# A two-part transformer kernel: norms scaled on ScalarE and transposed on TensorE, conditioning sums in the experts' buffers, and the last norm's row spread through PSUM

## The chip, the cores and the metric

The kernel runs on one core of a Trainium2 chip. The core has five instruction streams that run side by side and wait for each other through semaphores: TensorE (PE in the profile, its weight loads PEld), VectorE (DVE), ScalarE (ACT), GpSimd (POOL) and SyncE (SP, which only issues transfers). Transfers run on 16 DMA engines. TensorE's clock has two levels, 1.2 and 2.4 GHz; the profile gives the granted clock of a stretch as a share of the full one. The metric is device time in microseconds (us) of one execution.

## The reference, cut to what matters

512 tokens of width 1024 go through two stacks, all in float32.

```
first_block:  for l in 0, 1:
    mod = silu(c) @ ada_w[l] + ada_b[l]            # six rows of 1024: shift, scale, gate (twice)
    hn  = rms_norm(h, g) * (1 + scale) + shift
    h   = h + gate * mixer_l(hn)                   # l = 0: gated recurrence, l = 1: stick-breaking attention
    hn  = rms_norm(h, g') * (1 + scale') + shift'
    h   = h + gate' * peer_ffn(hn)
    (after l = 0: keys and values from kv_ada_w, rms_norm and kv_w)
  return rms_norm(h, final_norm_g)

peer_ffn, each token: 64 experts e with weights gates[e], chosen by top-k over product keys
    hid[e] = xn . u[e];   out = sum_e gates[e] * gelu(hid[e]) * v[e]

second_block: hn = rmsnorm(x, g_pre) * (1 + scale) + shift;  proj = hn @ w_in
    mix = [gated_deltanet(proj), sparse_attention(proj)] @ w_out
    x   = x + gate * rmsnorm(mix, g_post)
```

## The kernel before, in words

The tokens are four blocks of 128, one token to a partition; `H[0]` to `H[3]` hold their residual rows of 1024. Stages run over pairs of blocks.

A **conditioning sum** (`ada`, 17 of them in the first 337 us) makes one row of 1024 from `silu(c)` and a 1024x1024 matrix: four loads of 1 MB into the ring of eight `g` buffers (`row2`), a multiply and seven multiply-adds of 128x1024 on DVE into the tile `acc`, of which there is one, and eight matmuls with a column of ones that add over the partitions into PSUM `ax`. DVE adds the bias to it.

A **norm** (`norm_T`, 24 calls: six stages by four blocks) takes the reciprocal root mean square of a block on ACT (`rms`), multiplies the identity by it on DVE (tile `dg`, a diagonal matrix), and multiplies eight 128x128 pieces of the residual by that matrix on PE, which transposes and scales at once. ACT then scales and shifts the pieces out of PSUM into the projections' operand.

A **peer block** (`peer(l, b)`) gathers for each of 64 experts a row of u and v (1 MB for 128 tokens, by GpSimd's indirect transfer, into a `g` buffer), takes the dot product with u on DVE, gelu on ACT for four experts at a time, and adds the weighted v either on DVE (tile `acc`) or on PE (a diagonal `dgv` made on ACT, then two 128x512 matmuls into PSUM `vp`); `PE_SLOTS` says how many go to PE. At the end `acc` and `vp` are added, multiplied by the gate, which is spread over the partitions by diagonals and matmuls with ones into `ax`, and added to `H[b]`. A buffer of the ring comes free for the next gather once its v is used. Each pair of peer blocks is merged with the other stages' work for other blocks: the mixers, the next norms, keys and values, and beside the last pair the second stack for blocks 0, 1 and 2. The second stack of block 3 is the tail.

`spread` puts a gate row on all partitions in the same way as above, with diagonals from DVE. `second_norm` multiplies a block by its root mean square and by the row `final_norm_g`, which is loaded to all partitions by two transfers on SP into two of the six `t2` buffers, and then calls `norm_T`. `dsa_attend` multiplies the softmax numerators by a diagonal of 1/sum on PE, which transposes them.

The order of work on SP is that of the program. The order on the other engines is chosen when the program is built, by a list scheduler, so that moved lines of code don't say by themselves how the engines' orders move.

Of the kernel before, what the change touches and what calls it, by code (L numbers as in the profile page):

```python
# [12 lines left out]
I32 = mybir.dt.int32  # L13
# [7 lines left out]
D = 1024  # L21
KC = 8
NB = 4
# [14 lines left out]
PE_SLOTS = {(0, 0): 16, (0, 1): 32, (0, 2): 28, (0, 3): 24, (1, 0): 24, (1, 1): 24, (1, 2): 20, (1, 3): 24}  # L38
# [71 lines left out]
def kernel(ctx: ExitStack, tc: tile.TileContext, a, at, out):  # L110
# [163 lines left out]
    def norm_T(src, ga, sh, dst, t0, wide=None):  # L274

        r = rms(src, D)
        dg = S("dg" if wide is None else "dgv", [128, 128], bufs=3 if wide is None else 2)
        ts(dg, ident, r, OP.mult)
        yield
        for half in range(2):  # L280
            p = mmt() if wide is None else wide[:, half * 512:half * 512 + 512]
            for j in range(4):
                k = 4 * half + j
                mm(p[:, j * 128:(j + 1) * 128], src[:, k * 128:(k + 1) * 128], dg)
            for j in range(4):
                k = 4 * half + j
                act(dst[:, k, t0:t0 + 128], p[:, j * 128:(j + 1) * 128], AF.Identity,
                    scale=ga[:, k:k + 1], bias=sh[:, k:k + 1])
            yield
# [31 lines left out]
    def ada(cact, name, i, bias, dst):  # L321

        acc = S("acc", [128, D], bufs=ACC_BUFS)
        for k in range(KC):
            if k % 2 == 0:
                two = row2().rearrange("p (j n) -> p j n", j=2)
                loads[-1].dma_start(two, a[name][i, k * 128:k * 128 + 256].rearrange("(j p) n -> p j n", p=128))
            w = two[:, k % 2]
            if k:
                stt(acc, w, cact[:, k:k + 1], acc, OP.mult, OP.add)  # L330
            else:
                ts(acc, w, cact[:, 0:1], OP.mult)
            yield
        p = axt()
        for j in range(8):
            mm(p[:, j:j + 1], acc[:, j * 128:j * 128 + 128], one)
        tt(dst, p[:, :8], bias, OP.add)
        yield

    def spread(cols, dst):  # L340

        for half in range(2):
            p = axt()
            for j in range(4):
                dg = S("dg", [128, 128], bufs=3)
                ts(dg, ident, cols[:, 4 * half + j:4 * half + j + 1], OP.mult)
                mm(p[:, j * 128:(j + 1) * 128], C["ones"], dg)
            A.copy(dst[:, half * 512:half * 512 + 512], p)
            yield

# [200 lines left out]
    def route_pick(l, b, qT, xT, kb, m=4):  # L551
# [7 lines left out]
        idx = S("idx", [128, 4, 16], I32, bufs=3)  # L559
        gt = S("gt", [128, 4, 16], bufs=3)  # L560
# [83 lines left out]
    def peer(l, b, cols):  # L644
# [3 lines left out]
        on_pe = [((e + 1) * npe) // 64 > (e * npe) // 64 for e in range(64)]  # L648
        hid = S("hid", [128, 64], bufs=2)
# [4 lines left out]
        rows = {}  # L654
        for s in range(64 + GROUP):
            if s < 64:
# [8 lines left out]
            e = s - GROUP  # L665
            if e < 0:
                yield
                continue
            if e % GROUP == 0:
                g = slice(e, e + GROUP)  # L670
                tt(w[:, g], w[:, g], gt[:, g], OP.mult)
            t = rows.pop(e)[:, D:]
            if on_pe[e]:
                dg = S("dgv", [128, 128], bufs=2)
                act(dg, ident, AF.Copy, scale=w[:, e:e + 1])
                left -= 1
                for half in range(2):
                    sl = slice(half * 512, half * 512 + 512)
                    mm(vp[:, sl], dg, t[:, sl], first_p, left == 0)
                first_p = False  # L680
            elif first_d:
                ts(acc, t, w[:, e:e + 1], OP.mult)
                first_d = False
            else:
                stt(acc, t, w[:, e:e + 1], acc, OP.mult, OP.add)
            yield
        if (l, b) == (1, NB - 1):
            for half in range(2):
                sl = slice(half * 512, half * 512 + 512)
                tt(acc[:, sl], acc[:, sl], vp[:, sl], OP.add)  # L690
        else:
            tt(acc, acc, vp, OP.add)
        for half in range(2):
            sl = slice(half * 512, half * 512 + 512)
            p = axt()
            for j in range(4):
                dg = S("dg", [128, 128], bufs=3)
                act(dg, ident, AF.Copy, scale=cols[:, 4 * half + j:4 * half + j + 1])
                mm(p[:, j * 128:(j + 1) * 128], C["ones"], dg)
            tt(acc[:, sl], acc[:, sl], p, OP.mult)  # L700
# [127 lines left out]
    def second_norm(b, t0, hT):  # L828
        fg = [t2(), t2()]
        for half in range(2):  # L830
            sl = slice(half * 512, half * 512 + 512)
            SP.dma_start(fg[half], a["final_norm_g"][sl].unsqueeze(0).to_broadcast([128, 512]))
        r = rms(H[b], D)
        for half in range(2):
            sl = slice(half * 512, half * 512 + 512)
            stt(H[b][:, sl], H[b][:, sl], r, fg[half], OP.mult, OP.mult)
# [133 lines left out]
    def dsa_attend(b, d, qbT, zbs, mix):  # L970
        N = 128 * (b + 1)
        for h in range(4):
# [17 lines left out]
            dg = S("dg", [128, 128], bufs=3)  # L990
            ts(dg, ident, s, OP.mult)
            yield
            p = pot()
            for j in range(b + 1):
                mm(p[:, j * 128:(j + 1) * 128], l[:, j * 128:(j + 1) * 128], dg)
# [467 lines left out]
def lay(inputs):  # L1463
# [21 lines left out]
    for n, src in (("c", "c"), ("c_2", "c_2"), ("norm_mix_g", "norm_mix_g"), ("lb", "hgrn_lb_logits"),  # L1485
                   ("onorm", "hgrn_onorm_g"), ("norm_ffn_g", "norm_ffn_g"), ("kv_ada_b", "kv_ada_b"),
                   ("kv_norm_g", "kv_norm_g"), ("b_ada_2", "b_ada_2"), ("g_pre", "g_pre_2"), ("ada_b", "ada_b"),
                   ("g_post", "g_post_2"), ("conv", "conv_w_2"), ("g_gdn", "g_gdn_2")):
# [31 lines left out]
```

## Time and profile before

| | us |
|---|---|
| median of 3 runs | 2449.67 (2448.4 to 2451.24) |
| the profiled execution | 2450.95 |
| its span | 2449.2 |
| PE busy | 1882.7 (77%) |
| DVE busy | 1786.6 (73%) |
| ACT busy | 758.7 (31%) |
| POOL busy | 673.8 (28%) |

The mean granted clock of TensorE is 0.871. Busy is the time in which an engine executed something, over the whole program; the 767 MB that the transfers moved are 313 GB/s on average. Six stretches are told apart below by time: 0 to 312 us, before the first gather; 312 to 798, with peer blocks (0,0) and (0,1); 798 to 1222, with (0,2) and (0,3); 1222 to 1658, with (1,0) and (1,1); 1658 to 2290, with (1,2), (1,3) and the second stack of blocks 0 to 2; and the tail.

### The profile page before, as it was taken

The numbers are of one execution on the slowest core, as the hardware profiler recorded it, in microseconds if no ns is written. First come the engines' busy times: TensorE is split into PE (matmuls) and PEld (weight loads), VectorE is DVE, ScalarE is ACT, GpSimd is POOL, SyncE is SP. The second block draws the span as 40 slices with busy tenths as digits, with TensorE's granted clock in tenths as the row PEclk, the third lists the DMA queues.
The fourth block names the chain that finished last, engine by engine and source line by source line (L and its number), as shares of the span: only waits on it lengthen the run. The fifth ranks groups of instructions, "written<-read, shape, count | busy, mean of one in ns | idle before, by whom it ended". The sixth has DMA issues, their size and how long they took to land.

```text
span 2449.2 us, 25291 instructions
## 1 busy us (share of the span) xinstructions
PE 1882.7 (77%) x8832; PEld 1375.8 (56%) x8832; DVE 1786.6 (73%) x3772; ACT 758.7 (31%) x1601; POOL 673.8 (28%) x516
## 2 busy tenths in 40 slices
PE   5996859977945997784489887547996788974698
PEld 4984748853721784462168565315774465742484
DVE  5677887789698737879862786996768656777573
ACT  2331213343211335431133553114223324322232
POOL 0000013344335415433630443442213212132000
PEclk9998869988977999887799998766999888976799
DMA  9978657998889989998996999897867628957630
GB/s 388 367 299 323 260 206 310 421 362 338 364 332 404 398 311 394 382 380 321 395 378 275 368 408 358 346 373 279 340 242 273 232 112 312 385 212 282 262 129 18
DMA packets 123990, 767.38 MB, mean 313 GB/s; under 512 B 12468, under 2 KB 19636, under 8 KB 40792
## 3 DMA queue, kind: packets, MB, share of 16 engines
q0 software_dynamic: 73728, 536.90, 55.2%
q1 hardware_dynamic: 39952, 198.01, 20.6%
q10 hardware_dynamic: 10184, 30.86, 3.4%
q8 instruction: 70, 1.15, 0.2%
q14 instruction: 56, 0.46, 0.0%
HBM read 763.62 MB, written 2.11 MB: 313 GB/s over the span
## 4 chain that ended last, share of the span: by engine, by line
PE 45%; DVE 24%; DMA 13%; issue 11%; ACT 4%; POOL 3%; SPq 0%; ACTq 0%; POOLq 0%; DVEq 0%
PE mm L156 28%; DMA g<-in_peer_uv_dram,idx 11%; PE vp L156 7%; DVE acc L168 7%; DVE g L168 7%; PE ax L156 6%; PE po L156 4%; POOL g L658 3%; DVE arena L159 2%; ACT t L150 1%; ACT L146 1%; ACT arena L150 1%; DVE t L159 1%; DMA arena<-bscr 1%; DVE arena L517 1%
## 5 line engine op out<-in xcount | busy, mean ns | idle before, releaser
L658 POOL DMA_INDIRECT g<-in_peer_uv_dram,idx x512 | 673.6, 1316 | 1594.8 <-DVE acc L168 623.1
L168 DVE SCALAR_TENSOR_TENSOR g<-g,xn 128x1024 f32<-128x1024 f32 x512 | 620.8, 1219 | 249.0 <-DMA g<-in_peer_uv_dram,idx 237.8
L156 PE MATMUL vp<-g,dgv 128*128 128x512 f32 x768 | 447.2, 726 | 277.1 <-ACT dgv L150 277.0
L156 PE MATMUL mm<-arena,w 128*128 128x128 f32 (+1 forms) x3696 | 621.5, 326 | 3.0 <-ACT arena L150 2.9
L156 PEld LDWEIGHTS mm<-arena,w 128*128 128x128 f32 x3696 | 554.5, 192 | 71.8 <-issue 23.9
L156 PEld LDWEIGHTS vp<-g,dgv 128*128 128x128 f32 x768 | 169.2, 233 | 486.9 <-ACT dgv L150 316.3
L168 DVE SCALAR_TENSOR_TENSOR acc<-g,pw,acc 128x1024 f32<-128x1024 f32 x312 | 399.4, 1280 | 4.4
L156 PE MATMUL mm<-w,arena 128*128 128x256 f32 (+2 forms) x800 | 249.5, 464 | 11.5 <-DVE arena L159 4.7
L146 ACT ACT_TABLE_LOAD x171 | 219.4, 1283 | 4.7 <-PEq L1516 1.7
L156 PEld LDWEIGHTS mm<-w,arena 128*128 128x128 f32 x800 | 150.7, 196 | 95.9 <-issue 65.3
L168 DVE SCALAR_TENSOR_TENSOR acc<-g,cac,acc 128x1024 f32<-128x1024 f32 x119 | 152.4, 1281 | 5.7 <-DMA g<-in_ada_w_dram 3.6
L150 ACT ACTIVATE pw<-hid 128x4 f32<-128x4 f32 x128 | 26.0, 205 | 418.8 <-DVE g L168 417.8
L150 ACT ACTIVATE dgv<-cst,pw 128x128 f32<-128x128 f32 x192 | 70.3, 396 | 53.3 <-DVE pw L159 33.7
L156 PE MATMUL mm<-dg,h 128*128 128x128 f32 x368 | 57.9, 317 | 37.3 <-DVE dg L163 30.0
L156 PEld LDWEIGHTS mm<-dg,h 128*128 128x128 f32 x368 | 53.9, 228 | 44.9 <-DVE dg L163 32.9
L156 PE MATMUL po<-arena 128*128 128x128 f32 (+1 forms) x400 | 67.6, 299 | 7.0 <-DVE arena L429 3.8
L156 PE MATMUL ax<-one,acc 128*128 128x1 f32 x272 | 40.1, 277 | 42.1 <-DVE acc L168 41.4
L150 ACT ACTIVATE arena<-mm,msh,msc 128x128 f32<-128x128 f32 x128 | 48.0, 464 | 66.7 <-PE mm L156 29.8
L156 PEld LDWEIGHTS po<-arena 128*128 128x128 f32 x400 | 58.5, 208 | 16.3 <-DVE arena L429 4.5
L156 PEld LDWEIGHTS ax<-one,acc 128*128 128x128 f32 x272 | 40.2, 233 | 45.2 <-DVE acc L168 24.9
L150 ACT ACTIVATE t<-po 128x512 f32<-128x512 f32 (+3 forms) x80 | 37.0, 470 | 83.0 <-PE po L156 81.8
L159 DVE TENSOR_TENSOR pw<-pw,gt 128x4 f32<-128x4 f32 x128 | 20.1, 159 | 57.8 <-ACT pw L150 57.3
(269 smaller groups left out, 2068.4 us busy)
## 6 DMA issues: line engine op xcount, KB each, us to landing
g<-in_ada_w_dram SPq DMA_DIRECT2D x44, 1024.0 KB
w<-in_w_in_dram SPq DMA_DIRECT2D x42, 1024.0 KB
w<-in_hgrn_w_in_dram SPq DMA_DIRECT2D x30, 1024.0 KB
w<-in_peer_w_q_dram SPq DMA_DIRECT2D x16, 1024.0 KB
w<-in_kv_w_dram SPq DMA_DIRECT2D x16, 1024.0 KB
g<-in_w_ada_dram ACTq DMA_DIRECT2D x12, 1024.0 KB
w<-in_hgrn_w_out_dram SPq DMA_DIRECT2D x8, 1024.0 KB
g<-in_kv_ada_w_dram ACTq DMA_DIRECT2D x8, 1024.0 KB
```

The lines of the kernel that those rows point to most:

```text
L146: ld = A.preload_act_table_set(s)
L150: i = A.activation(out_, in_, fn, **kw)
L156: T.matmul(o, lhsT, rhs, start=start, stop=stop, **kw)
L159: V.tensor_tensor(o, x, y, op=op)
L168: V.scalar_tensor_tensor(o, x, s, y, op0=op, op1=op2, **kw)
L517: V.match_replace(w, best[:, 0:8], src, MARK)
L658: G.indirect_dma_start(out=t, out_offset=None, in_=uv_rows, in_offset=bass.IndirectOffsetOnAxis(ap=idx[:, s:s + 1], axis=0))
```

## The change

- `norm_T` scales the block on ACT (two copies of 128x512 with the root mean square as scale, into two `t2` buffers) and transposes the eight pieces on PE with the identity. The diagonal on DVE goes. `dsa_attend` does likewise: ACT multiplies by 1/sum, PE transposes.
- `ada` takes a buffer of the `g` ring in place of `acc`, so that two sums can be open at once and the loads have fewer buffers.
- `spread` makes its diagonals on ACT.
- `second_norm` no longer loads `final_norm_g`; it is held as eight columns and spread by four diagonals on ACT and four matmuls with ones for each half (`over_partitions`) into `ax`, which DVE reads.
- `peer` is written with an expert's v sum ahead of the next u dot. The last peer block sends 27 experts to PE (26 by `PE_SLOTS`, and the last two always) where it sent 24, spreads its gate ahead of time into two `t2` buffers, adds the DVE part to `H[3]` first and the PE part behind it. The other blocks add `acc` and `vp` in halves.
- `idx` and `gt` get four buffers for three, `dgv` three for two; the scratch of the indirect transfers is 2048 where it was 4096.

```
-PE_SLOTS = {..., (1, 2): 20, (1, 3): 24}
+PE_SLOTS = {..., (1, 2): 20, (1, 3): 26}
...
     def norm_T(src, ga, sh, dst, t0, wide=None):
         r = rms(src, D)
-        dg = S("dg" if wide is None else "dgv", [128, 128], bufs=3 if wide is None else 2)
-        ts(dg, ident, r, OP.mult)
+        xs = [t2(), t2()]
+        for half in range(2):
+            act(xs[half], src[:, half * 512:half * 512 + 512], AF.Copy, scale=r)
         yield
         for half in range(2):
             p = mmt() if wide is None else wide[:, half * 512:half * 512 + 512]
             for j in range(4):
-                k = 4 * half + j
-                mm(p[:, j * 128:(j + 1) * 128], src[:, k * 128:(k + 1) * 128], dg)
+                T.transpose(p[:, j * 128:(j + 1) * 128], xs[half][:, j * 128:(j + 1) * 128], ident)
...
     def ada(cact, name, i, bias, dst):
-        acc = S("acc", [128, D], bufs=ACC_BUFS)
+        acc = row2()[:, :D]
...
+    def over_partitions(cols, half):
+        p = axt()
+        for j in range(4):
+            dg = S("dg", [128, 128], bufs=3)
+            act(dg, ident, AF.Copy, scale=cols[:, 4 * half + j:4 * half + j + 1])
+            mm(p[:, j * 128:(j + 1) * 128], C["ones"], dg)
+        return p
...
     def peer(l, b, cols):
+        if (l, b) == (1, NB - 1):
+            on_pe = [x or e >= 62 for e, x in enumerate(on_pe)]
+            npe = sum(on_pe)
...
+            elif last and s < 66:
+                gate.append(t2())
+                A.copy(gate[-1], over_partitions(cols, s - 64))
         for half in range(2):
             sl = slice(half * 512, half * 512 + 512)
+            if last:
+                tt(acc[:, sl], acc[:, sl], gate[half], OP.mult)
+                tt(H[b][:, sl], H[b][:, sl], acc[:, sl], OP.add)
+                tt(acc[:, sl], vp[:, sl], gate[half], OP.mult)
+            else:
+                tt(acc[:, sl], acc[:, sl], vp[:, sl], OP.add)
+                tt(acc[:, sl], acc[:, sl], over_partitions(cols, half), OP.mult)
             tt(H[b][:, sl], H[b][:, sl], acc[:, sl], OP.add)
...
     def second_norm(b, t0, hT):
-        fg = [t2(), t2()]
-        for half in range(2):
-            sl = slice(half * 512, half * 512 + 512)
-            SP.dma_start(fg[half], a["final_norm_g"][sl].unsqueeze(0).to_broadcast([128, 512]))
         r = rms(H[b], D)
         for half in range(2):
             sl = slice(half * 512, half * 512 + 512)
-            stt(H[b][:, sl], H[b][:, sl], r, fg[half], OP.mult, OP.mult)
+            p = over_partitions(vecs["final"], half)
+            yield
+            stt(H[b][:, sl], H[b][:, sl], r, p, OP.mult, OP.mult)
...
-            dg = S("dg", [128, 128], bufs=3)
-            ts(dg, ident, s, OP.mult)
+            act(l[:, :N], l[:, :N], AF.Copy, scale=s)
             yield
             p = pot()
             for j in range(b + 1):
-                mm(p[:, j * 128:(j + 1) * 128], l[:, j * 128:(j + 1) * 128], dg)
+                T.transpose(p[:, j * 128:(j + 1) * 128], l[:, j * 128:(j + 1) * 128], ident)
```

Three places in the engines' orders follow. The first is DVE at the start of the program: the end of the first conditioning sum and the second and third, `msh10` and `msc10` being the finished rows. Before:

```order
L168 SCALAR_TENSOR_TENSOR acc_104<-g_117,cac_83,acc_104 128x1024 x2
L159 TENSOR_TENSOR msh10_103<-ax_121,vcols_72 128x8
L163 TENSOR_SCALAR acc_132<-g_133,cac_83 128x1024
L168 SCALAR_TENSOR_TENSOR acc_132<-g_133,cac_83,acc_132 128x1024
L168 SCALAR_TENSOR_TENSOR acc_132<-g_137,cac_83,acc_132 128x1024 x2
```

And of the change:

```order
L168 SCALAR_TENSOR_TENSOR g_104<-g_117,cac_83,g_104 128x1024 x2
L163 TENSOR_SCALAR g_132<-g_133,cac_83 128x1024
L168 SCALAR_TENSOR_TENSOR g_132<-g_133,cac_83,g_132 128x1024
L159 TENSOR_TENSOR msh10_103<-ax_121,vcols_72 128x8
L168 SCALAR_TENSOR_TENSOR g_132<-g_137,cac_83,g_132 128x1024 x2
```

The second sum's first two instructions now stand ahead of the row that reads the first sum's matmuls (`ax_121`). The second place is DVE inside peer block (0,2), where `pw` is the four experts' weights, `hid` marks a u dot and `acc` a v sum. Before:

```order
L159 TENSOR_TENSOR pw_3914<-pw_3914,gt_3385 128x4
L168 SCALAR_TENSOR_TENSOR acc_3915<-g_4259,pw_3914,acc_3915 128x1024
L168 SCALAR_TENSOR_TENSOR g_4361,hid_3913<-g_4361,xn_3563 128x1024
L168 SCALAR_TENSOR_TENSOR acc_3915<-g_4282,pw_3914,acc_3915 128x1024
L168 SCALAR_TENSOR_TENSOR acc_3915<-g_4330,pw_3914,acc_3915 128x1024
L168 SCALAR_TENSOR_TENSOR g_4376,hid_3913<-g_4376,xn_3563 128x1024
```

And of the change:

```order
L159 TENSOR_TENSOR pw_3931<-pw_3931,gt_3399 128x4
L168 SCALAR_TENSOR_TENSOR acc_3932<-g_4291,pw_3931,acc_3932 128x1024
L168 SCALAR_TENSOR_TENSOR g_4396,hid_3930<-g_4396,xn_3578 128x1024
L168 SCALAR_TENSOR_TENSOR acc_3932<-g_4316,pw_3931,acc_3932 128x1024
L168 SCALAR_TENSOR_TENSOR acc_3932<-g_4367,pw_3931,acc_3932 128x1024
L168 SCALAR_TENSOR_TENSOR g_4412,hid_3930<-g_4412,xn_3578 128x1024
```

The kinds of instructions stand in the same order in both. The third place is ACT where the last peer block ends and the tail's norm begins (`h3_71` is `H[3]`). Before:

```order
L146 ACT_TABLE_LOAD
L150 ACTIVATE dgv_11124<-cst_74,pw_9740 128x128
L150 ACTIVATE dgv_11129<-cst_74,pw_9740 128x128
L150 ACTIVATE t2_11169,rms_11170<-h3_71 128x1024
L150 ACTIVATE rms_11170<-rms_11170,eps_66 128x1
L150 ACTIVATE rms_11170<-rms_11170 128x1
L150 ACTIVATE t2_11178,rms_11179<-h3_71 128x1024
L150 ACTIVATE rms_11179<-rms_11179,eps_66 128x1
L150 ACTIVATE rms_11179<-rms_11179 128x1
L150 ACTIVATE arena_65<-vp_11177,msh2nd_1368,mA2nd_1470 128x128 x8
```

And of the change:

```order
L146 ACT_TABLE_LOAD
L150 ACTIVATE dgv_11249<-cst_74,pw_9803 128x128
L150 ACTIVATE dgv_11268<-cst_74,pw_9803 128x128
L150 ACTIVATE dgv_11272<-cst_74,pw_9803 128x128
L150 ACTIVATE t2_11284,rms_11285<-h3_71 128x1024
...
L150 ACTIVATE rms_11320<-rms_11320 128x1
L150 ACTIVATE t2_11324<-h3_71,rms_11320 128x512
L150 ACTIVATE t2_11325<-h3_71,rms_11320 128x512
L150 ACTIVATE arena_65<-vp_11318,msh2nd_1374,mA2nd_1476 128x128 x8
```

A third diagonal has come in for the last four experts, and the two scaled copies stand right behind the root mean square, where before the next thing was the evacuation of PE's products.

## Rows read from the trace of the kernel before

**Rows 1.** The chain that ended last: shares of the span by engine.
```profile
PE 45%; DVE 24%; DMA 13%; issue 11%; ACT 4%; POOL 3%; SPq 0%; ACTq 0%; POOLq 0%; DVEq 0%
```

**Rows 2.** Windows by stage: length, busy of five engines, granted clock, DMA share, GB/s.
```profile
0.00:312.00 312.00, 249.37 (x1331) 212.73 (x1332) 215.07 (x326) 79.56 (x156) 0.20 (x4) 0.93 0.84 325
312.00:798.00 486.00, 357.31 (x1519) 252.44 (x1517) 404.88 (x1016) 133.48 (x261) 182.42 (x135) 0.84 0.86 344
798.00:1222.00 424.00, 312.37 (x1303) 210.32 (x1304) 315.32 (x673) 142.29 (x323) 173.00 (x129) 0.87 0.92 368
1222.00:1658.00 436.00, 333.26 (x1516) 234.85 (x1514) 324.33 (x676) 159.66 (x324) 166.54 (x128) 0.87 0.90 359
1658.00:2290.00 632.00, 493.11 (x2278) 355.78 (x2277) 440.61 (x876) 194.34 (x429) 151.64 (x121) 0.84 0.70 272
2290.00:2449.00 159.00, 137.28 (x892) 109.70 (x891) 86.37 (x207) 49.37 (x109) 0.00 (x0) 0.95 0.26 92
```

**Rows 3.** Timeline of DVE, 24 to 338 us: instructions that waited for conditioning sums' matmuls.
```profile
25.07 0.17 DVE L159 TENSOR_TENSOR msh<-ax,vcols 128x8 f32<-128x8 f32 x1 [3.66 <-PE ax L156]
...
247.29 0.17 DVE L159 TENSOR_TENSOR mg<-ax,vcols 128x8 f32<-128x8 f32 x1 [3.73 <-PE ax L156]
...
316.68 0.17 DVE L159 TENSOR_TENSOR mA2nd<-ax,vcols 128x8 f32<-128x8 f32 x1 [4.32 <-PE ax L156]
```

**Rows 4.** Timeline of PE: a norm's products, 41 us; v sums, then transposes, 674 us.
```profile
41.39 3.78 PE L156 MATMUL mm<-dg,h 128*128 128x128 f32 x16 [2.61 <-ACT arena L150]
...
673.96 2.74 PE L156 MATMUL vp<-g,dgv 128*128 128x512 f32 x6
676.54 1.04 PE L546 MATMUL ax<-cst,arena 128*128 128x128 f32 x8
```

**Rows 5.** Groups: line, engine, operation, count; busy, mean ns of one; idle before.
```profile
L168 DVE SCALAR_TENSOR_TENSOR acc<-g,cac,acc 128x1024 f32<-128x1024 f32 x119 | 152.4, 1281 | 5.7 <-DMA g<-in_ada_w_dram 3.6
L150 ACT ACTIVATE dgv<-cst,pw 128x128 f32<-128x128 f32 x192 | 70.3, 396 | 53.3 <-DVE pw L159 33.7
L156 PE MATMUL mm<-dg,h 128*128 128x128 f32 x368 | 57.9, 317 | 37.3 <-DVE dg L163 30.0
```

**Rows 6.** ACT's groups with shapes apart, columns as in Rows 5: a scaled copy.
```profile
L150 ACT ACTIVATE t<-t,one 128x512 f32<-128x512 f32 x8 | 5.5, 712 | 0.1
```

**Rows 7.** Waits: who waited for whom, us in total, times, longest.
```profile
PE vp L156 <- ACT dgv L150: 277.0, 52, 14.2
...
DVE pw L159 <- ACT pw L150: 57.3, 71, 12.9
```

**Rows 8.** Timeline, 2028 to 2051 us: SP, DVE and PE at block 2's last norm.
```profile
2028.84 0.99 SPq L832 DMA_DIRECT2D t<-in_final_norm_g_dram  x2
...
2046.42 1.41 DVE L168 SCALAR_TENSOR_TENSOR h<-h,rms,t 128x512 f32<-128x512 f32 x2
...
2049.61 0.29 DVE L163 TENSOR_SCALAR dg<-cst,rms 128x128 f32<-128x128 f32 x1 [1.78 <-ACT rms L150]
2049.95 1.44 PE L156 MATMUL mm<-dg,h 128*128 128x128 f32 x5 [6.60 <-DVE dg L163]
```

**Rows 9.** Timeline, 2284 to 2302 us: the last peer block ends, the tail begins.
```profile
2284.38 5.95 PE L156 MATMUL vp<-g,dgv 128*128 128x512 f32 x8 [10.35 <-ACT dgv L150]
2290.37 1.28 DVE L159 TENSOR_TENSOR acc<-acc,vp 128x512 f32<-128x512 f32 x2 [4.92 <-PE vp L156]
...
2292.77 1.28 DVE L159 TENSOR_TENSOR h<-h,acc 128x512 f32<-128x512 f32 x2
...
2299.02 0.29 DVE L163 TENSOR_SCALAR dgv<-cst,rms 128x128 f32<-128x128 f32 x1 [1.78 <-ACT rms L150]
2299.36 2.08 PE L156 MATMUL vp<-dgv,h 128*128 128x128 f32 x8 [9.03 <-DVE dgv L163]
2301.47 1.51 ACT L150 ACTIVATE arena<-vp,msh2nd,mA2nd 128x128 f32<-128x128 f32 x4 [2.49 <-PE vp L156]
```

**Rows 10.** Window of PE's transposes of 676 us, columns as in Rows 2.
```profile
676.50:677.60 1.10, 1.07 (x9) 0.80 (x7) 0.61 (x1) 0.00 (x0) 0.00 (x0) 1.00 1.08 454
```

## What the change will do

> **What bounds the kernel now.** I read the chain that ended last first. PE holds 45% of it and DVE 24%, transfers 13%, ACT 4% [rows 1]: no single engine is the limit, work changes hands between PE and DVE, and a microsecond that is taken off one of them shortens the program only where that engine holds the chain at that moment. The windows by stage say which engine that is [rows 2]. Before 312 us PE is busy 249 of 312 us. From 312 to 1658 us the transfers are busy 0.86 to 0.92 of the time, so gathers stand close behind whatever else is the limit, and DVE is busiest in the first of the three stretches (405 of 486 us). From 1658 to 2290 us PE leads with 493 of 632 us and the transfers fall to 0.70. In the tail PE is busy 137 of 159 us. ACT is never busy for more than 37% of a stretch (159.66 of 436 us), and that is where the change puts work.
>
> The timelines then show what the changed places wait for. At 25.07 us DVE has been idle for 3.66 us because the single sum tile is still being read by PE, and this comes again later, 3.73 us at 247 and 4.32 us at 317 [rows 3]. A norm's sixteen PE rows (float32 products take two rows each) took 3.78 us at 41 us, while eight transposes of the same size took 1.04 us [rows 4].
>
> **The start, to 312 us.** The second sum can begin when the first ends and not 3.66 us later, if its loads are there; the order on DVE shows its first instructions ahead of the wait. The norm of the second block falls from 3.78 us to some 1.04 us on PE [rows 4], which is full from there on, so that up to 3.66 + 2.74 = 6.4 us are gained by 52 us. Behind 240 us DVE and PE take turns, and the waits of 3.73 and 4.32 us can go as well, 14.5 us in all. Against that the sum's tile takes a buffer of the ring. With two sums open, six loads are ahead in place of eight, so a load waits for two more loads' use, four multiply-adds of 1.281 us = 5.1 us [rows 5], and SP's weight loads behind it in the queue wait too. That bounds the start from -14.5 to +5. I take **-8**: the first 6.4, which lie where PE has no gap to lose them in, and a fifth of the 8.1 behind.
>
> **The norms and the attention, 312 us to the tail.** A norm's products cost PE 57.9 / 23 = 2.52 us on average [rows 5]; transposes 1.04 [rows 4]: -1.48 us. Two norms are counted at the start and one in the tail, so 21 remain: -31 us of PE work. `dsa_attend` has 40 rows of 80 less, at 57.9 / 368 = 0.157 us each -6 us, and the spreading of the final row adds 64 rows, +10 us. PE does 27 us less; weighted by its 45% of the chain this is -12 us. The latency of a norm moves the other way: ACT's first copy (0.712 us, the nearest row with a scale operand [rows 6]) stands where DVE's diagonal (0.29 us [rows 8]) stood, +0.42 us, while the second copy lies beside the first four transposes. Over 21 norms by the same share: +4 us. DVE loses 64 diagonals of 0.29 us, 24 of norms, 24 of `spread`, 16 of attention, and three multiply-adds of 1.28 us: -22 us of work, by its 24% -5 us. Sum -13; because the transfers are busy for nine tenths of the time from 312 to 1658 us and take back part of what the engines gain, I take **-11**. The bounds are 0 (all of it waits for gathers) and -53 (31 + 22, all on the path); no row supports the second, since PE and DVE would have to hold the chain by turns exactly there.
>
> **Final norm of block 2.** The loads of the row are issued at 2028.84 us, well before the multiplication at 2046.42, so that their landing is not what it waits for; behind it PE waits 6.60 us for DVE's diagonal, which itself waited for the root mean square [rows 8]. The loads that go save transfers of no weight, and the wait stays but for the difference of copies and transposes above. I cost this edit at nothing; what covers it is that the residual of block 2 is normalised late for other reasons, and if the row's landing did decide, 2046.42 - 2028.84 = 17.6 us is the most that it could give back.
>
> **v sums ahead of u dots.** The order on DVE within a peer block has the same sequence of kinds before and after, so the scheduler undoes the rewriting: nothing. If it did come through, each of 128 groups of four would meet the gelu one dot earlier, on top of the 57.3 us that DVE waits for gelu now [rows 7].
>
> **The buffers and the scratch.** More `idx`, `gt` and `dgv` buffers take waits away only; the halved scratch I cost at nothing, since no row shows GpSimd waiting for it; this is an open cost and belongs to the range.
>
> **The end of the peer blocks and the tail.** Three experts stand on PE behind the last gelu where two did: twelve rows in place of eight, at 5.95 / 8 = 0.744 us +3.0 us [rows 9], or at the full clock of 2.74 / 6 = 0.457 us a row [rows 4] 5.5 in place of 5.95 us, -0.5. I take +2. After PE's end DVE has three pairs of halves to do, from 2290.37 to 2292.77 + 1.28 = 2294.05 us [rows 9]; now two pairs, since the gate and the DVE part are done before: a third of 3.7 us, -1.2. The norm's first half took 2.45 us from the diagonal to the evacuation (2299.02 to 2301.47 us); a copy of 0.71 and four transposes at half clock, 1.04 us, make some 1.8: -0.6, and as much again for the second half. Sum **-0.5**, between -3 and +2.
>
> **The sum.** -8 - 11 - 0.5 = -19.5 us from the profiled execution's 2450.95 us (1.3 above the median of 2449.67): 2431.5, which I give as **2432 us**.
>
> **The rivals.** *The gathers hide it* (0.15). Then only the start's 6 us are left: 2445 us. For it: 0.86 to 0.92 of transfer time over 1346 us. Against it: the chain has transfers for 13% alone.
>
> *More is on the path* (0.17): all 14.5 us at the start and 27 us of PE work: 2409 us. For it: PE's 45%, and 493 of 632 us in the longest stretch.
>
> *ACT gets late* (0.11), which ends on the other side. ACT gets 48 copies of 0.71 and 56 diagonals of 0.40 us, 56 us of work. It runs in order, and queued behind the copies are gelus and the diagonals `dgv`, for which PE already waits 277.0 us and DVE 57.3 us [rows 7]. If both copies of each of 21 norms, 1.42 us, push the path back, that is +30 us against -19.5: 2461 us. It decides from the point at which two norms in three delay a gelu or a `dgv` that something waits for. Against it: ACT is busy for under 37% of any stretch, and DVE's waits for gelu are 0.8 us each.
>
> *The clock falls behind the transposes* (0.04). If a stretch of transposes did not keep PE's clock up, the sixteen rows behind each norm would run at 0.744 and not 0.457 us, 4.6 us for each of 21 norms, by 45% +43 us: 2475 us. The one stretch of eight transposes that I looked at ran at a granted clock of 1.00, with v sums at full speed ahead of it [rows 4, 10]; it is too short to exclude the rival. The Trainium skill states such a rule in "TensorE: Matmul & The Clock Gate", Part 4: PE-mode transpose, by which the full clock does not engage for transposes since they don't count as busy in the same way. By that rule, and the trace of before agrees only as far as a clock that was up did not drop within 1.04 us, a norm would no longer raise the clock for the projection behind it.
>
> **How the numbers follow.** The forecast gets 0.53. The range reaches from 2408, where "more" lies, to 2455: the start's bound of +5 in place of -8 and a tail of +2 give 2447, and half of what ACT could cost another 8. Outside are most of ACT (0.08), the clock (0.04) and a tail of "more" (0.06). A measurement here tells about 0.2%, 4.9 us, from no change. Faster: 0.52 of the forecast, 0.17 of "more" and 0.05 of "hidden", 0.74. Same: 0.10 of "hidden" and 0.02: 0.12. Slower: ACT, the clock, less their overlap with no change: 0.14.
>
> **What would show it.** In the profile after, DVE's waits for `ax` before 312 us should shrink and the second sum start before 23 us; norms should show eight PE rows in about 1 us; the peer blocks should end earlier, the first by some 8 us, the last by about 19, its v sums on PE at 2271 us in place of 2284.38 + 5.95 = 2290.3. A longer wait of PE for `dgv` or of DVE for `pw` would show the ACT rival; a granted clock below 0.871 the clock rival; the same ends of peer blocks with more idle time on DVE the hidden case. The prediction is wrong if the new orders put something late that I have not priced, or if the loads at the start come later by more than the sums gain.

## The result, and the profile after

The changed kernel takes 2423.6 us (median of 4 runs, 2415.86 to 2428.8) where the kernel before took 2449.03 beside it: a ratio of 0.990, 95% interval 0.9878 to 0.9923. It is faster by some 25 us where 17 were forecast, and inside the range. The profiled execution has a span of 2419.0 us. The chain that ended last, by engine, answers to [rows 1]:

```profile
span 2419.0 us, 24977 instructions
...
PE 42%; DVE 22%; issue 14%; DMA 13%; ACT 5%; POOL 4%; POOLq 0%; ACTq 0%; DVEq 0%
```

The windows by stage, cut at the same events as in [rows 2] (the first gather, and the start of the addition of `acc` and `vp` in peer blocks (0,1), (0,3), (1,1) and (1,3)), columns as there:

```profile
0.00:299.00 299.00, 251.81 (x1378) 214.11 (x1379) 226.12 (x360) 91.47 (x180) 0.20 (x4) 0.95 0.88 344
299.00:758.00 459.00, 339.75 (x1411) 234.96 (x1410) 389.71 (x964) 133.52 (x263) 182.79 (x135) 0.85 0.89 362
758.00:1182.00 424.00, 304.41 (x1251) 204.85 (x1250) 313.53 (x663) 148.01 (x340) 176.71 (x129) 0.85 0.91 365
1182.00:1614.00 432.00, 332.09 (x1471) 230.35 (x1469) 322.97 (x668) 164.52 (x332) 175.57 (x129) 0.87 0.91 361
1614.00:2258.00 644.00, 501.73 (x2307) 360.17 (x2305) 437.08 (x861) 219.39 (x493) 149.55 (x122) 0.85 0.69 266
2258.00:2419.00 161.00, 139.00 (x869) 109.75 (x867) 83.75 (x200) 53.65 (x115) 0.00 (x0) 0.93 0.25 90
```

Against the lengths in [rows 2] the stages changed by -13, -27, 0, -4, +12 and +2 us. The whole gain stands in the first two, and the stage with the second stack gives 12 us of it back. To compare all kernels below by the same events, this table has the times at which each thing happened in the profiled executions: the start of the last conditioning sum, the ninth u dot of block (0,0), the last u dots of (0,0), (1,1) and (1,3), the first finished projection (`nat`) of the second stack, and the span.

| kernel | last sum | 9th dot | (0,0) | (1,1) | first `nat` | (1,3) | span | median of all runs |
|---|---|---|---|---|---|---|---|---|
| before | 316.8 | 383.6 | 578.2 | 1647.8 | 1704.0 | 2281.1 | 2449.2 | 2449.03 |
| changed | 279.3 | 352.3 | 545.7 | 1604.9 | 1670.9 | 2247.9 | 2419.0 | 2423.6 |
| e1, sums in one tile | 330.9 | 397.4 | 592.3 | 1653.7 | 1721.6 | 2298.7 | 2469.1 | 2470.87 |
| e2, ring alone | 281.0 | 354.1 | 546.5 | 1618.1 | 1674.3 | 2244.3 | 2417.9 | 2417.07 |
| e3, norm alone | 332.4 | 398.9 | 591.0 | 1659.7 | 1698.7 | 2292.8 | 2463.7 | 2467.15 |
| e3b, norm undone | 280.7 | 352.8 | 547.8 | 1610.7 | 1675.9 | 2270.7 | 2439.0 | 2449.31 |
| e9, ring and norm | 281.9 | 354.3 | 546.8 | 1612.4 | 1649.3 | 2246.9 | 2417.4 | 2419.66 |
| e4, row loaded | 281.7 | 354.3 | 550.5 | 1609.9 | 1643.1 | 2235.4 | 2400.9 | 2399.42 |
| e8, final row, DVE | 280.0 | 352.4 | 550.2 | 1615.9 | 1682.9 | 2267.1 | 2432.6 | 2435.48 |
| e6, last block plain | 279.5 | 353.2 | 548.5 | 1621.3 | 1687.9 | 2258.6 | 2428.4 | 2429.71 |
| f10, row in `po` | 280.0 | 353.2 | 547.9 | 1612.1 | 1679.1 | 2259.8 | 2429.9 | 2431.49 |
| f13, gate row first | 279.1 | 354.2 | 549.6 | 1612.8 | 1659.5 | 2242.1 | 2414.6 | 2428.8 |
| f11, loaded, u first | 282.7 | 355.4 | 547.8 | 1613.7 | 1650.7 | 2247.5 | 2421.0 | 2421.51 |
| f12, two tiles | 284.1 | 356.4 | 553.4 | 1673.0 | 1724.5 | 2306.4 | 2473.6 | 2485.09 |

Between jobs the median of the kernel before moved from 2444.4 to 2449.0 us, so ratios decide, each against runs of the kernel before on the same chip. In e3b, f12 and f13 the profiled execution was the fastest of its runs, 9 to 12 us below the median, so that their times in the table flatter them.

The start after the change, on DVE's timeline, answers to [rows 3]:

```profile
21.36 0.75 DVE L163 TENSOR_SCALAR g<-g,cac 128x1024 f32<-128x1024 f32 x1
22.15 1.28 DVE L168 SCALAR_TENSOR_TENSOR g<-g,cac 128x1024 f32<-128x1024 f32 x1
25.11 0.17 DVE L159 TENSOR_TENSOR msh<-ax,vcols 128x8 f32<-128x8 f32 x1 [1.68 <-PE ax L156]
...
36.75 0.17 DVE L159 TENSOR_TENSOR msc<-ax,vcols 128x8 f32<-128x8 f32 x1 [2.13 <-PE ax L156]
...
279.30 0.74 DVE L163 TENSOR_SCALAR g<-g,cac 128x1024 f32<-128x1024 f32 x1
```

The second sum starts at 21.36 us, but DVE still waits 1.68 us for the first one's matmuls, because the reading row stands two instructions behind. The last sum starts at 279.30 us, 37 us earlier than before. PE's timeline at the second block's norm answers to the 3.78 us of [rows 4]:

```profile
39.84 1.11 PE L284 MATMUL mm<-cst,t 128*128 128x128 f32 x4 [3.13 <-ACT arena L150]
41.24 1.11 PE L284 MATMUL mm<-cst,t 128*128 128x128 f32 x4 [0.28 <-ACT arena L150]
42.64 9.12 PE L156 MATMUL mm<-arena 128*128 128x256 f32 x32 [0.28 <-ACT arena L150]
51.60 8.58 PE L156 MATMUL mm<-arena,w 128*128 128x256 f32 x39
```

And before, behind the norm's products:

```profile
45.07 7.81 PE L156 MATMUL mm<-arena 128*128 128x256 f32 x32
52.71 20.88 PE L156 MATMUL mm<-arena,w 128*128 128x256 f32 x96
```

PE waits for ACT's evacuations between the halves and its projections begin at 42.64 and not at 41.39 + 3.78 = 45.2 us: 2.5 us and not 6.4. Of these only 1.1 us are left where the next rows begin, at 51.60 in place of 52.71 us. The windows give a granted clock of 1.00 for this time, but the rows themselves show the lower level: in the changed kernel the projection's rows start 0.43 us apart until 46.2 us and 0.22 us apart from 46.6 us on, and in the kernel before the change of pace comes at 46.4 us too. The changed kernel spent its lead on rows at the slow pace. For the same reason four transposes took 1.11 us here, while the 1.04 us for eight in [rows 4] were measured at a granted clock of 1.00 [rows 10].

### The profile page after: what moved, and what is told of

Same layout as the page of the kernel before. It is cut to its first block, busy times and chain, and to the rows that moved or that the text cites. A ratio compares the mean times of both kernels' runs of the same rounds, so it can differ in the third digit from the quotient of the medians.

```text
span 2419.0 us, 24977 instructions
## 1 busy us (share of the span) xinstructions
PE 1868.8 (77%) x8676; PEld 1354.2 (56%) x8676; DVE 1773.2 (73%) x3714; ACT 810.6 (34%) x1723; POOL 684.8 (28%) x516
## 4 chain that ended last, share of the span: by engine, by line
PE 42%; DVE 22%; issue 14%; DMA 13%; ACT 5%; POOL 4%; POOLq 0%; ACTq 0%; DVEq 0%
PE mm L156 25%; DMA g<-in_peer_uv_dram,idx 11%; DVE g L168 8%; PE vp L156 8%; PE ax L156 6%; DVE acc L168 5%; POOL g L692 4%; PE po L156 3%; DVE arena L159 1%; ACT L146 1%; ACT t L150 1%; DVE t L159 1%; ACT arena L150 1%; DVE arena L526 1%; DVE acc L159 1%
## 5 line engine op out<-in xcount | busy, mean ns | idle before, releaser
L692 POOL DMA_INDIRECT g<-in_peer_uv_dram,idx x512 | 684.6, 1337 | 1548.7 <-DVE acc L168 716.6
L156 PE MATMUL vp<-g,dgv 128*128 128x512 f32 x780 | 458.6, 733 | 255.1 <-ACT dgv L150 255.0
L168 DVE SCALAR_TENSOR_TENSOR g<-g,cac 128x1024 f32<-128x1024 f32 x119 | 152.5, 1281 | 13.5 <-DMA g<-in_ada_w_dram 6.8
L156 PE MATMUL ax<-dg,cst 128*128 128x128 f32 x240 | 44.3, 322 | 36.2 <-DVE arena L526 28.9
L159 DVE TENSOR_TENSOR pw<-pw,gt 128x4 f32<-128x4 f32 x128 | 20.1, 159 | 69.5 <-ACT pw L150 69.3
L284 PE MATMUL mm<-cst,t 128*128 128x128 f32 x184 | 32.4, 323 | 43.6 <-ACT t L150 29.2
L156 PEld LDWEIGHTS ax<-dg,cst 128*128 128x128 f32 x240 | 37.5, 214 | 49.8 <-DVE arena L526 30.8
L156 PE MATMUL ax<-t,arena 128*128 128x128 f32 x240 | 38.6, 295 | 23.6 <-ACT t L150 17.3
```

The source lines that it names most:

```text
L156: T.matmul(o, lhsT, rhs, start=start, stop=stop, **kw)
L159: V.tensor_tensor(o, x, y, op=op)
L168: V.scalar_tensor_tensor(o, x, s, y, op0=op, op1=op2, **kw)
L284: T.transpose(p[:, j * 128:(j + 1) * 128], xs[half][:, j * 128:(j + 1) * 128], ident)
L692: G.indirect_dma_start(out=t, out_offset=None, in_=uv_rows, in_offset=bass.IndirectOffsetOnAxis(ap=idx[:, s:s + 1], axis=0))
```

## The experiments

**Which part shortens the start.** Theory A: two open sums let DVE run them early. Theory B: the norms' transposes and what they take from DVE. First the changed kernel with one tile again:

```
     def ada(cact, name, i, bias, dst):
-        acc = row2()[:, :D]
+        acc = S("acc", [128, D], bufs=ACC_BUFS)
```

> The changed kernel with the conditioning sums back in the one tile acc and the ring's eight buffers for loads alone; all else of the change stays. Theory A (two open sums let VectorE run the 17 sums early, which is what shortened the start by some 30 us): the last sum starts again near 317 us and not 279, block (0,0)'s last u dot falls back by 20 us or more, and the total is 2440 to 2452 us. Theory B (the norms' transposes and the work taken from VectorE did it): 2418 to 2432 us, with the start as short as in the changed kernel.

2470.87 us, a ratio of 1.0104 (1.0072 to 1.0136): slower than before the change, and above both ranges. The start is back, and worse by 14 us than before; theory B, which expected it to stay short, falls. Then that part alone on the kernel before, the same line the other way round:

```
-        acc = S("acc", [128, D], bufs=ACC_BUFS)
+        acc = row2()[:, :D]
```

> The kernel before with this one part of the change: a conditioning sum takes a buffer of the g ring. Theory A: 2415 to 2430 us, nearly the whole gain, with the last sum's start near 280 us. Theory B: 2442 to 2452 us. If both parts are needed at once: about 2435 us.

2417.07 us, ratio 0.9879 (0.9839 to 0.992), the last sum at 281 us: this one line is worth the whole gain of the change. The ninth dot comes at 354.1 us, 1.8 us behind the changed kernel's, so that the norms add next to nothing to the start. Then the norms alone, `norm_T` of the change in the kernel before:

```
-        dg = S("dg" if wide is None else "dgv", [128, 128], bufs=3 if wide is None else 2)
-        ts(dg, ident, r, OP.mult)
+        xs = [t2(), t2()]
+        for half in range(2):
+            act(xs[half], src[:, half * 512:half * 512 + 512], AF.Copy, scale=r)
...
-                mm(p[:, j * 128:(j + 1) * 128], src[:, k * 128:(k + 1) * 128], dg)
+                T.transpose(p[:, j * 128:(j + 1) * 128], xs[half][:, j * 128:(j + 1) * 128], ident)
```

> The kernel before with this one part of the change: norms scaled on ScalarE and transposed on TensorE. Theory A: 2438 to 2450 us, since a norm's eight rows and the later start cancel for all but some 5 us. Theory B: 2418 to 2432 us.

2467.15 us, ratio 1.0078 (1.004 to 1.0116). Neither theory expected a loss. The last sum starts later by 16 us. On the way PE waited for a weight piece and DVE behind it for a sum's matmuls; PE's and DVE's timelines of e3:

```profile
150.91 2.47 PE L156 MATMUL mm<-w,arena 128*128 128x256 f32 x5 [4.94 <-DMA w<-in_hgrn_w_in_dram]
...
160.97 0.17 DVE L159 TENSOR_TENSOR msh<-ax,vcols 128x8 f32<-128x8 f32 x1 [9.98 <-PE ax L156]
```

On SP the weight pieces stand behind loads of the ring, which wait for sums, which wait for PE: with one tile the three engines hold each other up in turn. That is how I read these rows; no run separates it. The changed kernel with the norms' diagonals and scaled matmuls back, the lines of the last diff the other way round (three `dgv` tiles stay):

> The changed kernel with the norms' diagonals back on VectorE and the scaled matmuls back on TensorE. Theory A: 2420 to 2435 us. Theory B: 2438 to 2452 us.

2449.31 us, ratio 1.0011 (0.9986 to 1.0036): B's number, though the start is as short as in the changed kernel (352.8 us). Of the 20 us between the two spans 16 arise between the last u dots of (1,1) and (1,2), which lie 329.7 us apart in place of 313.7. Last, two tiles without using the ring, in the kernel before:

```
-GATHER_BUFS = 8
+GATHER_BUFS = 7
-ACC_BUFS = 1
+ACC_BUFS = 2
```

> The kernel before with two tiles acc and a ring of seven buffers; nothing else is changed. Theory A (two sums open at once is what shortens the start): the last sum starts at 279 to 290 us and not 317, block (0,0)'s last dot comes at 545 to 560 us and not 578. If the ring's buffers as such are what mattered: 310 to 320 and 575 to 585. The total is worse than this gain by what one buffer less costs in the peer blocks, so it tells less: 2420 to 2450 us.

The last sum starts at 284 us and block (0,0) ends at 553: theory A. The seven buffers cost the peer stages more than that: from (0,0) to (1,1) it takes 1119.6 us where e2 takes 1071.6, and the total, 2485.09 us, ratio 1.0168 (1.011 to 1.0225), lies outside the range expected.

**What gives back 12 us at the second stack.** Theory C: ACT's diagonals for the final row. Theory D: the last peer block. The final row loaded, `second_norm` as before the change:

```
+        fg = [t2(), t2()]
+            SP.dma_start(fg[half], a["final_norm_g"][sl].unsqueeze(0).to_broadcast([128, 512]))
...
-            p = over_partitions(vecs["final"], half)
-            yield
-            stt(H[b][:, sl], H[b][:, sl], r, p, OP.mult, OP.mult)
+            stt(H[b][:, sl], H[b][:, sl], r, fg[half], OP.mult, OP.mult)
```

> The changed kernel with final_norm_g loaded to all partitions by transfers again, as before the change; all else of the change stays. Theory C (from block (1,1)'s last dot to the end the changed kernel needs 814 us where before it was 801, because ScalarE makes 24 diagonals in a row ahead of the second stack's first norms): this stretch returns to 800 to 806 us and the total is 2405 to 2418 us. Theory D (the new end of the last peer block and its 27 experts on TensorE cost it): the stretch stays at 812 to 818 and the total at 2419 to 2430 us.

2399.42 us, ratio 0.9797 (0.9769 to 0.9826): a gain beyond the expectation, and the fastest kernel here, ahead of the changed one's interval. PE at the second stack's first norms, in the changed kernel:

```profile
1630.24 2.08 PE L156 MATMUL ax<-arena 128*128 128x128 f32 x8 [4.84 <-DMA arena<-bscr]
...
1645.89 3.72 PE L156 MATMUL ax<-dg,cst 128*128 128x128 f32 x22 [0.29 <-ACT dg L150]
...
1652.80 1.27 PE L284 MATMUL mm<-cst,t 128*128 128x128 f32 x8 [1.28 <-ACT t L150]
1664.38 1.97 PE L284 MATMUL mm<-cst,t 128*128 128x128 f32 x8 [10.31 <-ACT t L150]
```

And in e4:

```profile
1620.49 1.27 PE L284 MATMUL mm<-cst,t 128*128 128x128 f32 x8 [1.53 <-ACT t L150]
...
1634.47 1.97 PE L284 MATMUL mm<-cst,t 128*128 128x128 f32 x8 [2.13 <-ACT t L150]
...
1651.30 3.78 PE L156 MATMUL ax<-arena 128*128 128x128 f32 x32
```

With the loaded row both norms' transposes stand ahead of the bias rows' matmuls (`ax<-arena`; the rows come back through DRAM, `arena<-bscr`); with the spread row they stand behind them. From the last dot of (1,1) to the first `nat` it takes 66 us with the spread row, 33 with the loaded one, 56 before. The diagonals on DVE, in `second_norm` alone:

```
-            p = over_partitions(vecs["final"], half)
+            p = axt()
+            for j in range(4):
+                dg = S("dg", [128, 128], bufs=3)
+                ts(dg, ident, vecs["final"][:, 4 * half + j:4 * half + j + 1], OP.mult)
+                mm(p[:, j * 128:(j + 1) * 128], C["ones"], dg)
```

> The changed kernel with the final row still spread through PSUM, but its diagonals made on VectorE (0.29 us each there, 0.33 to 0.40 on ScalarE). Theory C: VectorE is idle for some 6 us while TensorE waits for these diagonals, so that most of the 13 us come back: 2408 to 2419 us. If instead the TensorE rows of the spreading cost it: no change, 2419 to 2430 us.

2435.48 us, ratio 0.9951 (0.9932 to 0.9969), 67 us to the first `nat`: it is not who makes the diagonals. Theory C in this form falls. The time lies above both ranges, and the ratio above the changed kernel's interval. The last block as the others:

```
-        if (l, b) == (1, NB - 1):
-            on_pe = [x or e >= 62 for e, x in enumerate(on_pe)]
-            npe = sum(on_pe)
...
-            if last:
-                tt(acc[:, sl], acc[:, sl], gate[half], OP.mult)
-                tt(H[b][:, sl], H[b][:, sl], acc[:, sl], OP.add)
-                tt(acc[:, sl], vp[:, sl], gate[half], OP.mult)
-            else:
```

> The changed kernel with the last peer block treated like the others: 24 of its experts on TensorE, the gate spread at its end, no early addition to the residual. Theory C: the total stays at 2419 to 2430 us, the stretch from block (1,1)'s last dot at 810 us or more. Theory D: 2406 to 2418 us.

2429.71 us, ratio 0.9926 (0.9903 to 0.9949): theory D falls too. The new end is worth some 6 us by the medians, and the intervals overlap. The stretch from block (1,1)'s last dot is 807 us, so that theory C's 810 are not met either. Theory E: the spreading queues for PSUM `ax`. It goes to `po`:

```
-            p = over_partitions(vecs["final"], half)
+            p = over_partitions(vecs["final"], half, pot)
```

> The changed kernel with the final row still spread by ScalarE's diagonals and TensorE's ones, but into PSUM po instead of ax. Theory E (the spreading stands in line for ax behind the bias rows of the second stack, whose products wait 12 us for a transfer that comes back from DRAM): the first norm of the second stack no longer waits, from block (1,1)'s last dot to the first finished projection it takes 33 to 45 us instead of 66, and the total is 2395 to 2412 us, as with the loaded row. Theory C (ScalarE's diagonals or TensorE's extra rows themselves are the cost): 55 to 66 us, and 2415 to 2430 us.

2431.49 us, ratio 0.9945 (0.9923 to 0.9968), 67 us: falls. All diagonals share three `dg` tiles. Theory F: the gate row's diagonals hold them until the bias rows are through `ax`. ACT's timeline of the changed kernel doesn't show that:

```profile
1632.35 0.59 ACT L835 COPY arena<-ax 128x512 f32<-128x512 f32 x1 [10.79 <-PE ax L156]
...
1641.42 0.59 ACT L835 COPY arena<-ax 128x512 f32<-128x512 f32 x1 [2.09 <-PE ax L156]
1641.91 1.20 ACT L150 ACTIVATE dg<-cst,mgcol 128x128 f32<-128x128 f32 x3
```

ACT first copies the four bias rows out of PSUM and makes the gate row's first diagonals (`mgcol`) behind them; no `dg` is made in the 30 us ahead, and none in f10 either. So the gate row's diagonals are late by their place in ACT's order, and the final row's follow them. In e8, where DVE makes the final row's, its first one waits 4.92 us for PE, which works on the gate row's products: there the shared tiles can be the link. The gate row is spread ahead of the bias rows, with `po` as in f10:

```
-        (1, 2): [second_setup, lambda: row("g1row", "gcol"), lambda: second([0, 1]), ...],
+        (1, 2): [lambda: row("g1row", "gcol"), second_setup, lambda: second([0, 1]), ...],
```

> The changed kernel with the final row spread into po, and the second stack's gate row spread ahead of its bias rows where it was spread behind them. Theory F (all diagonals share three dg tiles; the gate row's hold them while its products wait for ax behind the bias rows, and these for a transfer from DRAM; whoever needs a dg next waits too): from block (1,1)'s last dot to the first finished projection it takes 33 to 48 us in place of 66, and the total is 2395 to 2414 us. If the diagonals and rows of the spreading themselves are the cost: 60 us or more, and 2418 to 2432 us.

PE's timeline of f13 has the first norm ahead of the bias rows:

```profile
1640.50 1.97 PE L284 MATMUL mm<-cst,t 128*128 128x128 f32 x8 [1.28 <-ACT t L150]
1647.10 4.63 PE L156 MATMUL ax<-arena 128*128 128x128 f32 x24 [4.62 <-DMA arena<-bscr]
```

The wait falls from 67 us in f10 to 47, as F expects. The median doesn't follow: 2428.8 us (2416.38 to 2433.36), ratio 0.9949 (0.9929 to 0.9968), though the profiled executions do, with spans of 2429.9 and 2414.6 us. So the gate row's place makes 20 of the 34 us by which f10 is behind e4 there; whether the three tiles or ACT's order alone do it is not shown, since no run has more `dg` tiles. The 24 us that the loaded row brings in the total are not explained by it.

**Ring and norm together**, the diffs of e2 and e3 in the kernel before, nothing else of the change:

> The kernel before with two parts of the change alone: sums in the ring's buffers, norms scaled on ScalarE and transposed. If the norm's transposes gain some 10 us in the peer stages once the ring has shortened the start, and the other parts cost 13 us at the second stack: 2402 to 2414 us. If the transposes gain nothing beside the ring: 2414 to 2422 us. If they cost what they cost alone, 22 us: 2435 to 2445 us.

2419.66 us, ratio 0.9889 (0.9865 to 0.9912). Beside the ring the transposes neither gain nor lose in the total, though with the loaded row they shorten the way to the first `nat` from 56 us (e2) to 37: what is gained there is given back by the last dot of (1,3). **v sums ahead of u dots**, undone in e4:

```
         for s in range(64 + GROUP):
+            if s < 64:
+                t = rows[s] = row2()
...
             e = s - GROUP
...
-            if s < 64:
-                t = rows[s] = row2()
```

> The changed kernel with final_norm_g loaded, and the peer loop written with the u dot ahead of the v sum again. If the scheduler undoes this rewriting, as its order on VectorE says: 2393 to 2408 us, as with the row loaded alone (2399). If v sums ahead of u dots free buffers earlier and gain: 2410 to 2425 us.

2421.51 us, ratio 0.9893 (0.9844 to 0.9942), 22 us slower than e4: the rewriting is not undone by the scheduler once the other parts are in. In the profiled executions the difference is 4 us at (1,1), 8 at the first `nat`, 12 at (1,3) and 20 at the end. The last 8 us lie behind the last dot, 6.4 of them behind the tail's first projection (145.6 and 139.2 us, at a granted clock of 0.93 and 0.98), where the peer loop no longer runs; they can't be put down to it by these rows. With e9 beside it f11 tells one thing more: it has all other parts of the change (`dsa_attend`, `spread`, the last block's end, the buffers, the scratch) on top of ring and norms, and the same ratio, so that these together bring nothing that the runs can tell.

## Why the prediction was right, and where it was not

The time was right in sign and range because errors cancelled, and that is luck.

- **The start, -8.** The mechanism was right, the size wrong by a factor of four: -31 us by the ninth dot (383.6 to 352.3). The step that failed is the bound: I added up DVE's waits for `ax` at the places where they stood (14.5 us with the shorter norm). A second tile also lets the scheduler put sums into other gaps of DVE, and a list of waits doesn't show these. The profile puts such a gap down to ACT in the kernel before, and the next sum begins only behind the row that reads the last one (`mg`):

```profile
68.01 0.69 DVE L159 TENSOR_TENSOR arena<-arena,t 128x512 f32<-128x512 f32 x1 [16.61 <-ACT t L150]
...
75.71 0.16 DVE L159 TENSOR_TENSOR mg<-ax,vcols 128x8 f32<-128x8 f32 x1
75.78 0.74 DVE L163 TENSOR_SCALAR acc<-g,cac 128x1024 f32<-128x1024 f32 x1
```

  In the changed kernel that sum begins in the gap:

```profile
57.80 0.75 DVE L163 TENSOR_SCALAR g<-g,cac 128x1024 f32<-128x1024 f32 x1 [6.12 <-DMA g<-in_ada_w_dram]
```

  The norm's 2.74 us was mis-sized too: it sets 3.78 us of the clock's lower level against 1.04 us of the full one. The feared cost of a narrower ring did not appear: in the change, e2 and f12 alike the last sum starts at 279 to 284 us.
- **The norms and the attention, -11.** From the end of block (0,0), -32.5 us, to that of (1,3), -33.2, nothing is gained in sum: -43 by the end of (1,1), and 10 given back. With ring and norm alone (e9) it comes to nothing as well. The price of PE's work was off: 184 transposes took 32.4 us, 1.41 us a norm, so that a norm saves 1.1 us and not 1.48:

```profile
L284 PE MATMUL mm<-cst,t 128*128 128x128 f32 x184 | 32.4, 323 | 43.6 <-ACT t L150 29.2
```

  Weighting a saving by an engine's share of the chain gave a number that no run supports.
- **The final row, nothing.** This step failed most. I looked at block 2 (the loads there were not waited for [rows 8]) and not at blocks 0 and 1, where the spread row puts the norms behind the bias rows. The loaded row makes the changed kernel 24 us faster; that this place is the reason is not shown, since f13 took 20 us off the wait and its median stayed, and e9 came 19 us earlier to `nat` than e2 with no gain in the end.
- **v sums ahead of u dots, nothing.** Wrong with the loaded row (22 us). I had compared orders before and after the whole change, and equal orders don't say that one edit is without effect, when another edit would have moved the same rows.
- **The tail, -0.5.** Right up to the first projection: from the last dot to `nat` 26.9 us in place of 27.8. Its terms, on the timeline after:

```profile
2251.16 7.32 PE L156 MATMUL vp<-g,dgv 128*128 128x512 f32 x12 [8.04 <-ACT dgv L150]
2258.52 1.29 DVE L159 TENSOR_TENSOR acc<-vp,t 128x512 f32<-128x512 f32 x2 [5.08 <-PE vp L156]
2259.73 1.28 DVE L159 TENSOR_TENSOR h<-h,acc 128x512 f32<-128x512 f32 x2
...
2265.97 1.33 ACT L150 ACTIVATE t<-h,rms 128x512 f32<-128x512 f32 x2
2266.75 1.11 PE L284 MATMUL vp<-cst,t 128*128 128x128 f32 x4 [8.26 <-ACT t L150]
2267.90 1.51 ACT L150 ACTIVATE arena<-vp,msh2nd,mA2nd 128x128 f32<-128x128 f32 x4 [0.59 <-PE vp L284]
```

  Twelve rows cost 7.32 - 5.95 = +1.4 us, the two pairs of halves -1.2, and from the copies to the evacuation it takes 1.93 in place of 2.45 us. Behind the first projection the prediction had nothing, and the tail took 4.0 us longer, at a granted clock of 0.95 where it was 0.99 (last section).
- **The rivals.** ACT did not get late on the whole: PE's waits for `dgv` fell from 277.0 to 255.0 us, DVE's for gelu rose from 57.3 to 69.3. The clock did not fall: 0.872 after, 0.871 before. In the tail the rows behind the norm came to the full pace (a pair of 128x144 in 0.41 us) 5.4 us after the first transpose, where before it was 7.0 us after the first product. The Trainium skill has a rule in "TensorE: Matmul & The Clock Gate", Part 4: PE-mode transpose, that transposes don't count as busy for the clock as other matmuls do; these rows neither bear it out nor exclude it, since eight transposes are a short stretch each time. The gathers hid nothing at the start, where the gain was. Behind block (0,0) it looks as that rival said: the way from its last dot to that of (1,3) took 1703 us before and 1702 after, and DVE waited longer for gathers; the first line is of the kernel before:

```profile
DVE g L168 <- DMA g<-in_peer_uv_dram,idx: 237.8, 139, 8.8
DVE g L168 <- DMA g<-in_peer_uv_dram,idx: 260.6, 154, 5.5
```

  That the gathers are the reason is not shown; e4 waits 264.7 us for them and is faster.
- **The range.** Its upper end adds 8 us as half of what ACT could cost; half of the 30 us that it names for ACT is 15, so that the sum as told ends at 2462 and not at 2455.

**Left open:** why the transposes cost 22 us alone, nothing beside the ring, and seem worth 25 with the whole change (e3b); and what of e4's 24 us lies beyond the local wait. In the profiled executions e4 is 18 us ahead: it is 5 us behind at (1,1), gains 17.6 by (1,3) and 5.5 in the tail, where its clock was higher. Open is also whether v sums ahead of u dots gain anything with the spread row. Each edit makes the scheduler choose other orders for all four engines, so a part's worth depends on the parts beside it.

## What to carry to other kernels

Where one accumulator is filled by one engine and read by another, a second one can be worth more than the waits at its hand-over (here 31 us against 14.5), since it frees the order of what stands around; it can be tried alone in one line. When a transfer is replaced by work on engines, ask which small rings (three diagonals, two PSUM tiles) it now shares and behind what it stands in an engine's order; the transfer that it replaced here had cost less. With an order chosen at build time, measure parts both alone and taken out: here the sum of the parts was not the whole.

## What the runs showed of the hardware

TensorE's granted clock can fall in a stretch in which PE hardly pauses. Windows of the tail at the same work, the changed kernel first (columns as in [rows 2]), then the kernel before:

```profile
2344.80:2354.80 10.00, 8.73 (x54) 6.49 (x52) 9.45 (x20) 1.76 (x3) 0.00 (x0) 1.00 0.00 0
2354.80:2364.80 10.00, 8.94 (x49) 7.39 (x50) 7.51 (x19) 1.18 (x2) 0.00 (x0) 0.80 0.01 2
2364.80:2374.80 10.00, 9.33 (x40) 7.03 (x40) 1.51 (x8) 4.98 (x10) 0.00 (x0) 0.69 0.00 0
```

```profile
2379.00:2389.00 10.00, 8.71 (x53) 6.46 (x52) 9.45 (x20) 1.76 (x3) 0.00 (x0) 1.00 0.01 2
2389.00:2399.00 10.00, 8.88 (x61) 7.27 (x62) 8.65 (x23) 1.99 (x4) 0.00 (x0) 1.00 0.00 0
2399.00:2409.00 10.00, 9.33 (x54) 6.78 (x52) 3.66 (x12) 4.97 (x10) 0.00 (x0) 1.00 0.01 2
```

With PE busy 8.73 of 10 us ahead of it in the one and 8.71 in the other, the clock fell to a mean of 0.80 and 0.69, toward its 1.2 GHz level, in the changed kernel and stayed at 2.4 GHz before. In the changed kernel PE pauses for no longer than 0.73 us from 2344.8 to 2360.6 us, as in the kernel before at the same work; then a pair of rows of 128x64 takes 0.69 us where it took 0.43. From the last `nat` to the end the changed kernel took 144.2 us and the kernel before 140.2; e4, with a mean clock of 0.98 there, 139.2.
